# Moving modulation splits, half a query rotation and a recurrence product from VectorE to ScalarE and GpSimd

## The chip, the cores and the metric

The kernel runs on 1 core of one Trainium2 chip. The metric is the device time of the whole program in microseconds (us), the median of three runs. Engines are named as the profile names them: PE (TensorE), PEld (its weight loads), DVE (VectorE), ACT (ScalarE), POOL (GpSimd), SP (SyncE, which issues all DMAs here).

## The reference

Two layers of a hybrid backbone over 256 context tokens and 1024 latent tokens. Cut to what the change touches:

```python
mod = SiLU(cond) @ w_ada + b_ada            # 1024 x 6144 weights, six parts per layer
h   = x * (1 + scale1) + shift1
z   = h @ w_in                              # "in-projection": q, k, v, xr, gr, zm
q   = _rmsnorm(q, q_g); k = _rmsnorm(k, k_g)
# rotary, latent tokens only
o = jnp.stack([x1 * cos - x2 * sin, x1 * sin + x2 * cos], -1)
# RG-LRU, forward and backward, 256 channels
log_a = -RG_C * softplus(-lam) * r          # r, i: sigmoids of two small matmuls of x
a = jnp.exp(log_a)
u = jnp.sqrt(-jnp.expm1(2.0 * log_a)) * i * x
h_t = a_t * h_(t-1) + u_t                   # associative scan
```

After the in-projection come block attention, the out-projection and a feed-forward stage; none of them is edited.

## The kernel before

All matmuls are done in three passes: each fp32 operand is split into a rounded part (`hi`) and the rest (`lo = x - hi`), and PE multiplies hi*hi, hi*lo and lo*hi (`mm3`, L173 to L175). `split` (L165 to L169) does it: a cast on ACT (L165) or DVE (L167), then a subtraction on POOL or DVE (L169).

The in-projection of a layer (`in_proj`) runs groups of columns in turn: xr and gr (the recurrence's input and gate), u and v of the gated MLP, k and v, then q. Three things run beside it as generators that the main line ticks forward:

- **The modulation stream, layer 0 only** (`ada_pe`): parts 2, 3 and 4 of `mod`, 48 slabs `araw` of 128x512 (two 128x256 weight pieces). Each slab is loaded by an SP DMA (L305), split into `ahi` and `alo`, and multiplied on PE (L173 to L175, L318, L319) by a four-column stationary operand. `araw` has two buffers, `ahi` and `alo` three each. The list `ASE` names the engines of the casts and subtractions of even and odd slabs. A new slab's DMA can be issued when the subtraction of the slab two before it has read its buffer.
- **The recurrence** (`lru`, `lru_unit`): per layer, two channel halves with a forward and a backward direction each, and one unit for the context tokens. After the sigmoids `R` and `G` (ACT, L849) come `G*x` on POOL (L855), tanh, exp, square on ACT, `T` on DVE (L866), the root on ACT (L870), `G = G*T` (L873), the scan on DVE (L877), the sum of both directions on POOL (L911) and the output product on DVE (L942). The convolution of the next channel half (L885, L889, tile `xc`, then its split `xh` and `xl`) stands between them on DVE.
- **q and k norms** (`qk_norm`): squares on ACT, a sum and an inverse root on DVE, then `qn` (L1070, from PSUM), the sine products `sq` (L1075, one per block `j` of a pair), the cosine product in place (L1079) and the sum (L1080). q has `nh` = 8 heads (a pair is 128x1024), k has 2. q runs over four latent pairs and one context pair per layer; `q_transpose` (L1137, L1142) follows.

A tile framework reorders the instructions by its own model of durations when the program is built: within an engine they then run in that fixed order. A wait at the head of an engine's queue holds everything behind it.

Of the kernel before, what the change touches and what calls it, by code (L numbers as in the profile page):

```python
# [12 lines left out]
ALU = mybir.AluOpType  # L13
# [44 lines left out]
QCH = ('q',)  # L58
KB = 2
ALAG = 2  # L60
ASE = (('dve', 'dve'), ('act', 'dve'))
XT = 5
CONVR = 0.6
CXP = (16, 17, 18, 19)
# [15 lines left out]
class Kern:  # L80
# [343 lines left out]
    def ada_pe(self, l, parts):  # L424
# [9 lines left out]
        for i in range(len(seq) + ALAG):  # L434
            if i + 1 < len(seq):
                raws.append(load(*seq[i + 1]))
            if i < len(seq):
                raw = raws.pop(0)
                sp.append([self.xs([P, 2, 256], F32R, s=s, bufs=ALAG + 1) for s in ("ahi", "alo")])
                self.split(*sp[-1], raw, *ASE[i % len(ASE)])  # L440
                del raw
# [391 lines left out]
    def lru_unit(self, l, dirs, xc, xh, xl, bd):  # L833

        nc = self.nc
        pf = self.pfm[l]
        bdh, bdl = bd
        RG = []
        for qs in dirs:
            RG.append((self.lx(s="R"), self.lx(s="G")))  # L840
            for gate, dst, bc in ((0, RG[-1][0], C_BA), (1, RG[-1][1], C_BX)):
                for q, cols, _, xs in qs:
                    j = (q * 2 + gate) % bdh.shape[1]
                    n = cols.stop - cols.start
                    for c0 in range(0, n, 512):
                        w = min(512, n - c0)
                        b = self.ps(tag="lg", bufs=2)
                        self.mm3(b[:, :w], bdh[:, j, :], bdl[:, j, :], xh[:, xs][:, c0:c0 + w], xl[:, xs][:, c0:c0 + w], True, True)
                        nc.scalar.activation(dst[:, cols][:, c0:c0 + w], b[:, :w], AF.Sigmoid, bias=pf[:, bc + q:bc + q + 1])  # L849
                        yield 0.6  # L850
        T = []
        for (R, G), qs in zip(RG, dirs):
            T.append(self.lx(s="T"))
            for q, cols, _, xs in qs:
                nc.gpsimd.tensor_tensor(G[:, cols], G[:, cols], xc[:, xs], ALU.mult)  # L855
                nc.scalar.activation(T[-1][:, cols], R[:, cols], AF.Tanh, scale=self.c8[l][:, 1, q:q + 1])
            yield 1.1
        for (R, G), qs in zip(RG, dirs):
            for q, cols, _, xs in qs:
                nc.scalar.activation(R[:, cols], R[:, cols], AF.Exp, scale=self.c8[l][:, 0, q:q + 1])  # L860
            yield 1.1

        for (R, G), t in zip(RG, T):
            sq = self.lx(s="sq")
            nc.scalar.activation(sq, R, AF.Square)
            nc.vector.scalar_tensor_tensor(t, sq, 1.0, t, ALU.add, ALU.mult)  # L866
            del sq
            yield 1.2
        for t in T:
            nc.scalar.activation(t, t, AF.Sqrt)  # L870
            yield 1.0
        for (R, G), t, qs in zip(RG, T, dirs):
            nc.vector.tensor_tensor(G, G, t, ALU.mult)  # L873
            yield 1.1
            for q, cols, init, xs in qs:
                v = [x[:, cols] if q % 2 == 0 else x[:, cols][:, ::-1] for x in (t, R, G)]
                nc.vector.tensor_tensor_scan(v[0], v[1], v[2], init, ALU.mult, ALU.add)  # L877
                yield (cols.stop - cols.start) / 900 + 0.1
        return T
# [173 lines left out]
    def qk_norm(self, bs, nh, gi, rope, t, scale, qn, sq):  # L1053


        nc = self.nc
        tabs, gg = rope
        n = nh * 64
        at = [slice(j * 2 // len(bs), (j + 1) * 2 // len(bs)) for j in range(len(bs))]
        for b, j in zip(bs, at):  # L1060
            nc.scalar.activation(sq[:, j, :], b, AF.Square)
        ss = self.sm([P, 2 * nh], s=f"ss{nh}", bufs=2)
        nc.vector.tensor_reduce(ss, sq.rearrange("p b (h d) -> p (b h) d", d=64), AX.X, ALU.add)

        nc.vector.tensor_scalar(ss, ss, RSC / (64 * scale * scale), RSC * EPS / (scale * scale), ALU.mult, ALU.add)
        r = self.rsqrt(ss, 2 * nh)
        q4 = qn.rearrange("p b (h d) -> p b h d", d=64)
        r4 = r.rearrange("p (b h) -> p b h", h=nh).unsqueeze(3).to_broadcast([P, 2, nh, 64])
        for b, j in zip(bs, at):
            nc.vector.tensor_tensor(q4[:, j], b.rearrange("p b (h d) -> p b h d", d=64), r4[:, j], ALU.mult)  # L1070
        if t >= 2:
            tb = slice((t - 2) * 64, t * 64)
            for j in range(2):
                sn = tabs[gi][:, 1, (t - 2 + j) * 64:(t - 1 + j) * 64].rearrange("p (i two) -> p i two", two=2)
                (nc.vector if j or nh == 2 else nc.gpsimd).tensor_tensor(sq[:, j, :].rearrange("p (h i two) -> p h i two", i=32, two=2),  # L1075
                                        qn[:, j, :].rearrange("p (h i two) -> p h i two", i=32, two=2)[:, :, :, ::-1],
                                        sn.unsqueeze(1).to_broadcast([P, nh, 32, 2]), ALU.mult)
            cs = tabs[gi][:, 0, tb].rearrange("p (b d) -> p b d", d=64).unsqueeze(2).to_broadcast([P, 2, nh, 64])
            nc.vector.tensor_tensor(q4, q4, cs, ALU.mult)  # L1079
            nc.vector.tensor_tensor(qn, qn, sq, ALU.add)  # L1080
        else:
            q3 = qn.rearrange("p b (h d) -> p (b h) d", d=64)
            nc.gpsimd.tensor_tensor(q3, q3, gg[:, gi, :].unsqueeze(1).to_broadcast([P, 2 * nh, 64]), ALU.mult)
        return qn
# [920 lines left out]
```

## Time and profile before

| | |
|---|---|
| median of 3 runs | 3202.53 us (3202.23 to 3202.85) |
| profiled execution | 3198.35 us, its span 3196.6 us |
| PE busy | 2978.1 us, 93% of the span |
| DVE busy | 2297.3 us, 72% |
| POOL busy | 1519.8 us, 48% |
| ACT busy | 1457.5 us, 46% |
| granted TensorE clock, mean | 0.974 |

The in-projections take the stretches from 64 to about 360 us (layer 0; the modulation stream runs from 64 to 220) and from about 1680 to 1905 us (layer 1). Busy shares are averages: what an engine's relief is worth is read from the stage in which it happens, from what PE waits for there. An instruction's duration in the trace includes time in which it had started and could not go on.

### The profile page before, as it was taken

Reading aid. Unit: us, or ns where it says so; the run is one execution under the profiler, and the core shown is the slowest. Engines: PE = TensorE matmul, PEld = TensorE weight load, DVE = VectorE, ACT = ScalarE, POOL = GpSimd, SP = SyncE. Lnnn points to the kernel's source line nnn. Section 1 sums busy time; section 2 is a strip of 40 time slices with the busy share of each in tenths; the row PEclk is TensorE's granted clock in tenths of the full one; section 3 lists DMA queues with packets and bytes.
Section 4 is the critical chain, followed back from the end, with each engine's and each line's share of the span. In section 5 each row is a group of like instructions: output and inputs, shape, how many; then the busy total and the mean of one; then the engine's idle time right before and its main releaser. Section 6 shows DMA issues by size and latency. Waiting matters only on the chain. (4 is left out here: it accounts for less than half of the span.)

```text
span 3196.6 us, 42662 instructions
## 1 busy us (share of the span) xinstructions
PE 2978.1 (93%) x15816; PEld 2487.5 (78%) x15816; DVE 2297.3 (72%) x4582; ACT 1457.5 (46%) x2236; POOL 1519.8 (48%) x850
## 2 busy tenths in 40 slices
PE   7888999999999999999899889999889999999993
PEld 5677789788888888788677868997668888888872
DVE  8879999766676634968664989986755452586859
ACT  5544578744333234332076438883344444433201
POOL 3322244503323227756733214358666666785675
PEclk9999999999999999999999999999989999999996
DMA  7331000235665645442321100004234553544231
GB/s 227 116 94 51 15 1 8 73 108 178 226 235 208 228 160 174 143 132 89 117 106 40 53 25 1 1 24 142 99 111 170 174 182 137 182 155 132 96 119 66
DMA packets 163392, 367.44 MB, mean 115 GB/s; under 512 B 20792, under 2 KB 58440, under 8 KB 163184
## 3 DMA queue, kind: packets, MB, share of 16 engines
q1 hardware_dynamic: 163184, 364.72, 33.5%
q8 instruction: 124, 2.03, 0.3%
q14 instruction: 84, 0.69, 0.1%
HBM read 261.84 MB, written 102.83 MB: 114 GB/s over the span
## 5 line engine op out<-in xcount | busy, mean ns | idle before, releaser
L169 POOL TENSOR_TENSOR wlo<-stg,whi 128x1024 fp32r<-128x1024 f32 (+2 forms) x116 | 240.3, 2084 | 420.8 <-ACT whi L165 381.8
L173 PE MATMUL ps<-hh,whi 128*128 128x512 f32 (+1 forms) x1040 | 376.2, 362 | 5.3 <-ACT htmp L567 4.5
L174 PE MATMUL ps<-hl,whi 128*128 128x512 f32 (+1 forms) x1040 | 374.2, 360 | 4.2 <-POOL hl L387 2.2
L175 PE MATMUL ps<-hh,wlo 128*128 128x512 f32 (+1 forms) x1040 | 373.4, 359 | 0.0
L175 PE MATMUL ps<-wh,ml 128*128 128x512 f32 x840 | 334.6, 398 | 0.0
L173 PE MATMUL ps<-wh,mh 128*128 128x512 f32 x840 | 330.3, 393 | 0.9 <-DVE accy L1749 0.9
L174 PE MATMUL ps<-wl,mh 128*128 128x512 f32 x840 | 330.8, 394 | 0.0
L169 POOL TENSOR_TENSOR pt<-ptf,pt 128x512 fp32r<-128x512 f32 x128 | 166.8, 1304 | 241.9 <-DVE pt L167 224.3
L169 DVE TENSOR_TENSOR ml<-mf,mh 128x1280 fp32r<-128x1280 f32 x84 | 178.2, 2121 | 121.9 <-ACT mh L165 99.2
L1176 DVE TENSOR_SCALAR_CACHE_REDUCE S<-sc 128x512 f32<-128x512 f32 (+1 forms) x416 | 224.8, 582 | 13.5 <-PE pT L1187 11.2
L165 ACT CAST mh<-mf 128x1280 fp32r<-128x1280 f32 x84 | 106.4, 1267 | 278.9 <-PE ps L174 234.7
L174 PEld LDWEIGHTS ps<-hl,whi 128*128 128x128 f32 x1040 | 196.8, 189 | 38.3 <-POOL hl L387 3.9
L173 PEld LDWEIGHTS ps<-hh,whi 128*128 128x128 f32 x1040 | 196.3, 189 | 38.3 <-ACT htmp L567 5.0
L169 POOL TENSOR_TENSOR wl<-wraw,wh 128x1024 fp32r<-128x1024 f32 x60 | 169.8, 2839 | 117.8 <-ACT wh L165 117.7
L175 PEld LDWEIGHTS ps<-hh,wlo 128*128 128x128 f32 x1040 | 197.5, 190 | 32.5
L1179 ACT ACTIVATE S<-S,anm 128x1280 f32<-128x1280 f32 (+1 forms) x160 | 191.2, 1196 | 38.2 <-DVE anm L1178 35.9
L1187 PE MATMUL pT<-ident,S 128*128 128x128 f32 x1344 | 202.2, 274 | 2.0 <-DVE pt L1196 1.4
L1212 PE MATMUL o<-pt,vt 128*128 128x256 f32 x1024 | 192.5, 303 | 9.8 <-POOL pt L169 7.9
L174 PE MATMUL ps<-slo,w1s 128*128 128x512 f32 x448 | 179.6, 401 | 13.8 <-DVE slo L169 13.7
L174 PEld LDWEIGHTS ps<-wl,mh 128*128 128x128 f32 x840 | 157.7, 188 | 40.3
L173 PEld LDWEIGHTS ps<-wh,mh 128*128 128x128 f32 x840 | 157.7, 188 | 39.4 <-DVE accy L1749 2.2
L175 PEld LDWEIGHTS ps<-wh,ml 128*128 128x128 f32 x840 | 157.7, 188 | 37.0
(393 smaller groups left out, 8471.7 us busy)
## 6 DMA issues: line engine op xcount, KB each, us to landing
mf<-mc SPq DMA_DIRECT2D x84, 640.0 KB
mc<-s SPq DMA_DIRECT2D x48, 640.0 KB
aslab<-in_w_ada SPq DMA_DIRECT2D x56, 512.0 KB
stg<-in_w_ff SPq DMA_DIRECT2D x48, 512.0 KB
wraw<-in_w_ff SPq DMA_DIRECT2D x48, 512.0 KB
mc<-f SPq DMA_DIRECT2D x72, 320.0 KB
w1r<-in_w_ff SPq DMA_DIRECT2D x32, 512.0 KB
stg<-in_w_in SPq DMA_DIRECT2D x28, 512.0 KB
```

Of the source, the lines that this page charges most:

```text
L165: nc.scalar.copy(hi, src)
L169: e.tensor_tensor(lo, src, hi.bitcast(F32), ALU.subtract)
L173: mm(out, lh, rh, start=start, stop=False)
L174: mm(out, lh, rl, start=False, stop=False)
L175: mm(out, ll, rh, start=False, stop=stop)
L1176: nc.vector.tensor_scalar(S[:, c0:c0 + n], b[:, :n], 1.0, -3.0e38, ALU.mult, ALU.max, accum_out=u["m"][:, hh, i:i + 1])
L1179: nc.scalar.activation(S[:, :c0], S[:, :c0], AF.Exp, bias=u["nm"][:, hh:hh + 1], accum_out=u["d"]["den"][:, ci % 2, hh:hh + 1])
L1187: nc.tensor.transpose(b[:, c, hh, :], u["S"][hh][:, (2 * j + c) * P:(2 * j + c + 1) * P], self.ident)
L1212: nc.tensor.matmul(o, v, pt[:, hl, c, :], start=j == 0 and c == 0 and hl == 0, stop=j == last and c == 1 and hl == 1)
```

## The change

Three edits. The modulation splits: even slabs are cast on ACT and subtracted on POOL (before: both on DVE); odd slabs stay as they were, cast on ACT and subtracted on DVE. The recurrence's product `G*T` goes from DVE to POOL in both layers. In the q rotation, the sine product of a pair's second block goes to POOL, where the first block's already was, and the sum is halved: the first block on POOL, the second on DVE. k is as before.

```diff
-ASE = (('dve', 'dve'), ('act', 'dve'))
+ASE = (('act', 'pool'), ('act', 'dve'))
...
         for (R, G), t, qs in zip(RG, T, dirs):
-            nc.vector.tensor_tensor(G, G, t, ALU.mult)
+            nc.gpsimd.tensor_tensor(G, G, t, ALU.mult)
...
-                (nc.vector if j or nh == 2 else nc.gpsimd).tensor_tensor(sq[:, j, :].rearrange("p (h i two) -> p h i two", i=32, two=2),
+                (nc.vector if nh == 2 else nc.gpsimd).tensor_tensor(sq[:, j, :].rearrange("p (h i two) -> p h i two", i=32, two=2),
...
-            nc.vector.tensor_tensor(qn, qn, sq, ALU.add)
+            if nh == 2:
+                nc.vector.tensor_tensor(qn, qn, sq, ALU.add)
+            else:
+                for e, j in ((nc.gpsimd, 0), (nc.vector, 1)):
+                    e.tensor_tensor(qn[:, j, :], qn[:, j, :], sq[:, j, :], ALU.add)
```

Since the framework orders the instructions anew, more moves than the diff names. Lines from L1083 on have numbers higher by 4 in the changed kernel.

POOL, layer 0, in the middle of the modulation stream (`wlo`: low part of in-projection weights; `xl`: low part of the convolution's result). Before:

```order
L169 TENSOR_TENSOR xl_885<-xc_799,xh_884 128x1024
L855 TENSOR_TENSOR G_898<-G_898,xc_799 128x1024
L169 TENSOR_TENSOR wlo_1266<-stg_784,whi_1265 128x1024
L855 TENSOR_TENSOR G_977<-G_977,xc_799 128x1024
L169 TENSOR_TENSOR wlo_1492<-stg_997,whi_1491 128x1024
L911 TENSOR_TENSOR T_1092<-T_1092,T_1122 128x1024
```

In the changed kernel, the same stretch from the second `G*x` on:

```order
L855 TENSOR_TENSOR G_977<-G_977,xc_799 128x1024
L169 TENSOR_TENSOR alo_1107<-araw_1083,ahi_1106 128x512
L169 TENSOR_TENSOR alo_1148<-araw_1125,ahi_1147 128x512
L169 TENSOR_TENSOR alo_1192<-araw_1165,ahi_1191 128x512
L873 TENSOR_TENSOR G_898<-G_898,T_1092 128x1024
L169 TENSOR_TENSOR alo_1230<-araw_1207,ahi_1229 128x512
L873 TENSOR_TENSOR G_977<-G_977,T_1122 128x1024
L911 TENSOR_TENSOR T_1092<-T_1092,T_1122 128x1024
L169 TENSOR_TENSOR alo_1278<-araw_1245,ahi_1277 128x512
L169 TENSOR_TENSOR wlo_1492<-stg_997,whi_1491 128x1024
```

The subtractions of the even slabs now stand between the recurrence's instructions; `alo_1278` stands behind L911, which needs the results of both scans on DVE.

DVE, layer 1, the first channel half's scans beside the convolution of the second half (`gr`, `cx`, `ug`: gate and MLP evacuations from PSUM banks `ps`). Before:

```order
L873 TENSOR_TENSOR G_15556<-G_15556,T_15649 128x1024
L205 SCALAR_TENSOR_TENSOR gr_15506<-gr_15506,ps_15699 128x512
L877 SCALAR_TENSOR_TENSOR T_15649<-R_15555,pfm_90,G_15556 128x1024
L873 TENSOR_TENSOR G_15593<-G_15593,T_15669 128x1024
L889 SCALAR_TENSOR_TENSOR xc_15814<-xr_15283,pfm_90,xc_15814 128x1023
L207 SCALAR_TENSOR_TENSOR gr_15506<-gr_15506,ps_15699 128x512
L205 SCALAR_TENSOR_TENSOR cx_15284<-cx_15284,ps_15739 128x256
L877 SCALAR_TENSOR_TENSOR T_15669<-R_15592,pfm_90,G_15593 128x1024
L207 SCALAR_TENSOR_TENSOR cx_15284<-cx_15284,ps_15739 128x256
L205 SCALAR_TENSOR_TENSOR ug_15770<-ug_15770,ps_15773 128x512
L889 SCALAR_TENSOR_TENSOR xc_15814<-xr_15283,pfm_90,xc_15814 128x1022
L942 SCALAR_TENSOR_TENSOR T_15649<-T_15649,gr_15505 128x1024
```

In the changed kernel:

```order
L877 SCALAR_TENSOR_TENSOR T_15653<-R_15559,pfm_90,G_15560 128x1024
L205 SCALAR_TENSOR_TENSOR gr_15510<-gr_15510,ps_15703 128x512
L877 SCALAR_TENSOR_TENSOR T_15673<-R_15596,pfm_90,G_15597 128x1024
L889 SCALAR_TENSOR_TENSOR xc_15818<-xr_15287,pfm_90,xc_15818 128x1023
L942 SCALAR_TENSOR_TENSOR T_15653<-T_15653,gr_15509 128x1024
L207 SCALAR_TENSOR_TENSOR gr_15510<-gr_15510,ps_15703 128x512
L205 SCALAR_TENSOR_TENSOR cx_15288<-cx_15288,ps_15743 128x256
L889 SCALAR_TENSOR_TENSOR xc_15818<-xr_15287,pfm_90,xc_15818 128x1022
```

Both products are gone, the second scan stands earlier, and L942, which needs POOL's L911, moved from behind the convolution's last step to two evacuations and that step's front.

DVE, layer 0, the last latent q pair. Before:

```order
L1070 TENSOR_TENSOR qn_3415<-ps_3380,rsy_566_3422 128x512
L1075 TENSOR_TENSOR sq_564_3416<-qn_3415,rtab_469_2643 128x512
L1142 TENSOR_TENSOR qT_3466<-qps_3467,qT_3466 64x4x128
L1079 TENSOR_TENSOR qn_3415<-qn_3415,rtab_469_2643 128x1024
L1142 TENSOR_TENSOR qT_3466<-qps_3467,qT_3466 64x4x128
L1080 TENSOR_TENSOR qn_3415<-qn_3415,sq_564_3416 128x1024
```

In the changed kernel:

```order
L1070 TENSOR_TENSOR qn_3418<-ps_3383,rsy_566_3425 128x512
L1146 TENSOR_TENSOR qT_3470<-qps_3471,qT_3470 64x4x128
L1079 TENSOR_TENSOR qn_3418<-qn_3418,rtab_469_2643 128x1024
L1146 TENSOR_TENSOR qT_3470<-qps_3471,qT_3470 64x4x128
L1084 TENSOR_TENSOR qn_3418<-qn_3418,sq_564_3419 128x512
```

The sine product left DVE, the cosine product now waits for two sine products of POOL, and the sum on DVE is half as wide.

## Rows read from the trace of the kernel before

**Rows 1.** Busy time by stage: window, length, busy (instructions), PE clock, DMA share, GB/s.

```profile
64.00:220.00 156.00, 131.82 (x778) 100.34 (x776) 122.86 (x167) 79.20 (x112) 47.29 (x21) 0.97 0.38 118
1760.00:1850.00 90.00, 75.22 (x531) 70.11 (x530) 85.51 (x271) 37.85 (x72) 23.44 (x18) 0.92 0.17 53
```

**Rows 2.** PE's waits, 64 to 220 us: total us, times, longest.

```profile
PE ada L318 <- DVE ahi L167: 8.8, 6, 2.6
PE ada L319 <- DVE alo L169: 3.0, 4, 1.3
PE adaf L326 <- DVE arow L461: 3.0, 3, 1.4
...
PE ada L174 <- DVE alo L169: 1.5, 2, 1.1
```

**Rows 3.** Slabs `araw`: instructions, duration min/median/max in ns, first and last start.

```profile
L305 SPq DMA_DIRECT2D araw<-in_w_ada x48: 367/368/546, 64.4 to 210.2; - x48
L169 DVE TENSOR_TENSOR alo<-araw,ahi x48: 654/691/2895, 74.4 to 217.4; 128x512 fp32r<-128x512 f32 x48
L167 DVE CAST ahi<-araw x24: 389/427/2640, 72.9 to 212.5; 128x512 fp32r<-128x512 f32 x24
L165 ACT CAST ahi<-araw x24: 600/618/623, 73.8 to 214.7; 128x512 fp32r<-128x512 f32 x24
```

**Rows 4.** SP's queue, 157 to 163 us: start, duration, issue (two slabs apart).

```profile
158.14 0.37 SPq L305 DMA_DIRECT2D araw<-in_w_ada  x1
...
162.13 0.37 SPq L305 DMA_DIRECT2D araw<-in_w_ada  x1
```

**Rows 5.** Groups by form, 64 to 220 us: busy us, mean ns, idle before and releasers.

```profile
L169 DVE TENSOR_TENSOR alo<-araw,ahi 128x512 fp32r<-128x512 f32 x48 | 44.1, 925 | 12.3 <-ACT ahi L165 11.9
...
L167 DVE CAST ahi<-araw 128x512 fp32r<-128x512 f32 x24 | 19.3, 802 | 11.3 <-DMA araw<-in_w_ada 9.7 <-PE ada L175 1.2
...
L855 POOL TENSOR_TENSOR G<-G,xc 128x1024 f32<-128x1024 f32 x4 | 9.8, 2440 | 34.5 <-ACT G L849 34.5
...
L873 DVE TENSOR_TENSOR G<-G,T 128x1024 f32<-128x1024 f32 x4 | 4.8, 1208 | 0.0
```

**Rows 6.** Timeline at 1794 us: start, duration, engine, instruction, idle before and releaser.

```profile
1794.45 2.35 POOL L169 TENSOR_TENSOR wlo<-stg,whi 128x1024 fp32r<-128x1024 f32 x1 [4.80 <-ACT whi L165]
1794.52 2.29 DVE L198 SCALAR_TENSOR_TENSOR rsy<-rst,rsy 128x2 f32<-128x2 f32 x1
```

**Rows 7.** Timeline, layer 1, first channel half's scans, 1710.5 to 1726 us.

```profile
1710.85 2.41 POOL L169 TENSOR_TENSOR wlo<-stg,whi 128x1024 fp32r<-128x1024 f32 x1 [5.02 <-ACT whi L165]
...
1711.20 4.20 DVE L877 TENSOR_TENSOR_SCAN T<-R,pfm,G 128x1024 f32<-128x1024 f32 x1
...
1718.57 2.34 DVE L877 TENSOR_TENSOR_SCAN T<-R,pfm,G 128x1024 f32<-128x1024 f32 x1
...
1721.05 2.38 POOL L911 TENSOR_TENSOR T<-T,T 128x1024 f32<-128x1024 f32 x1 [7.79 <-DVE T L877]
...
1721.74 2.78 DVE L889 SCALAR_TENSOR_TENSOR xc<-xr,pfm,xc 128x1022 f32<-128x1022 f32 x1
...
1724.44 1.21 DVE L942 SCALAR_TENSOR_TENSOR T<-T,gr 128x1024 f32<-128x1024 f32 x1
...
1725.64 0.51 PE L173 MATMUL ps<-xh,bdh 128*128 128x512 f32 x1 [2.90 <-ACT xh L165]
```

**Rows 8.** Timeline of the last latent q pair, layer 0, 349 to 356 us.

```profile
349.90 1.28 POOL L1075 TENSOR_TENSOR sq<-qn,rtab 128x512 f32<-128x512 f32 x1 [11.41 <-DVE qn L1070]
...
350.38 1.34 DVE L1075 TENSOR_TENSOR sq<-qn,rtab 128x512 f32<-128x512 f32 x1
...
352.48 1.23 DVE L1079 TENSOR_TENSOR qn<-qn,rtab 128x1024 f32<-128x1024 f32 x1
...
354.46 1.23 DVE L1080 TENSOR_TENSOR qn<-qn,sq 128x1024 f32<-128x1024 f32 x1
...
355.83 0.41 PE L1137 MATMUL qps<-ident,qn 128*128 128x128 f32 x2 [0.41 <-DVE qn L1080]
```

## The prediction

> **What bounds the kernel now.** I read the table of engines first: PE is busy 93% of the span, DVE 72%, so every microsecond gained or lost must come out of the 7% in which PE idles. Then the busy time by stage, since the edits act in two stretches only. In the modulation stretch (64 to 220 us) PE works 131.82 of 156 us and DVE 122.86, POOL only 47.29 [rows 1]: PE idles 24 us there, and DVE has 33 us left. In the middle of layer 1's in-projection (1760 to 1850) DVE works 85.51 of 90 us while PE has 75.22 [rows 1]: DVE is the fuller engine there. Third, PE's waits: in the modulation stretch 8.8 + 3.0 + 3.0 + 1.5 = 16.3 us end with a cast, a subtraction or the row sums of DVE [rows 2]. That is all that the first edit can win there through DVE. The stream itself also has to be looked at as a loop: 48 loads start between 64.4 and 210.2 us, 47 steps of 3.10 us, so one buffer turns over in 6.2 us [rows 3]. Where nothing disturbs it, a turn takes 162.13 - 158.14 = 3.99 us [rows 4]. So the buffers aren't the pace at present; casts and subtractions that come late are.
>
> Last, how DVE and POOL stand to each other, for two edits of three move work from the one to the other. At 1794.45 POOL starts a subtraction of 2.35 us, and at 1794.52 DVE starts an operation on 2 columns that takes 2.29 us [rows 6]: it ends when POOL's does. The scan at 1711.20 takes 4.20 us beside POOL's 2.41, and 2.34 later without [rows 7]. Such DVE operations wait out the POOL operation. The same shows in bulk: the 48 `alo` have a median of 0.69 us [rows 3] and a mean of 0.925 [rows 5], the 24 `ahi` 0.43 and 0.80. The excess is 44.1 - 48 x 0.69 = 11.0 and 19.3 - 24 x 0.43 = 9.0, together 20.0 us for 47.29 us of POOL work: DVE loses at least 0.42 us per us of POOL on these two groups alone.
>
> **The change part by part.** All terms are against the profiled execution's own 3198.35 us, 0.13% below the median of 3202.53; I add the 4.2 us at the end.
>
> *1. Modulation stretch.* Taken off DVE: 24 casts x 0.43 + 24 subtractions x 0.69 + 4 products x 1.21 = 10.3 + 16.6 + 4.8 = 31.7 us, at undisturbed durations [rows 3, 5]. Put on POOL: a subtraction of 128x512 isn't there on POOL before; by half of the 128x1024 rows (2.41 and 2.44, [rows 5, 7]) 1.2, and by the same width in the q rotation 1.28 [rows 8]; I take 1.28. So 24 x 1.28 + 4 x 2.44 = 40.5 us, and POOL goes from 47 to 88 of 156 us. What this takes back from DVE: at 0.42 per us 17 us, at one for one 40.5. I take 25, nearer the lower end because DVE isn't always there to be blocked, so DVE's net relief is about 7 us instead of 31.7. ACT gets 24 casts x 0.62 = 15 us more on 79 of 156; it has room.
>
> The even slabs pay for it: a cast of 0.62 for 0.43 and a subtraction of 1.28 for 0.69 make their way 0.8 us longer, 24 x 0.8 = 19 us if this length were the pace. It mostly isn't: 3.99 + 0.8 is still under 6.2. But POOL runs its list in order: in the new order four subtractions stand among the G products, and `alo_1278` stands behind the sum of directions, which waits for both scans; before, POOL idled 34.5 us ahead of its G products, waiting for sigmoids [rows 5], and nothing that PE needed soon stood behind them. Now slabs do. A late slab holds its `araw` buffer, the next load sits at the head of SP's queue, and weight loads sit behind it. Bounds: -16.3 (every wait of PE on DVE goes, nothing new) to +19 (the longer turn is the pace). Between them: the relief net of blocking is 7 of 31.7, so I credit 16.3 x 7/31.7 = -3.6; for new waits behind POOL's list I charge five late slabs at 1.28, +6.4, a choice. I take **+2**.
>
> *2. Layer 1's recurrence.* G*T takes 2.44 on POOL instead of 1.21 on DVE [rows 5]. The chain of a channel half is root, two products, two scans, sum, output product; the products now run one after the other on POOL, 4.88 for 2.42, and each also blocks the convolution steps or the first scan on DVE meanwhile: +2.4 on the chain. In the first half it then matters what stands ahead of what. Before, the last convolution step ran 1721.74 to 1724.52, stretched to 2.78 by the sum on POOL (2.38), and L942 came after it; the cast follows and PE waits 2.90 us for `xh` at 1725.64 [rows 7]. In the new order L942 stands ahead of that step: 1.21 us, and with it its wait for the sum on POOL, which the step before only overlapped. Together +2.4 + 1.2, with the step no longer stretched (1.28 instead of 2.78, -1.5 at most) but pushed behind the sum (up to 2.38): 0 to +6, I take +4. The second half falls in the stretch where DVE is 95% busy; there DVE gets 2.4 us back and the chain gets 2.4 longer: 0 to +3.5, and below zero if DVE's fill is what counts (-2.4); I take +2. The context unit, 128x256 columns, a quarter of it: +0.5. Sum **+6.5** (-3 to +10).
>
> *3. Layer 0's recurrence* lies within term 1; its context unit +0.5 (-1.2 to +1.2).
>
> *4. q rotation, eight latent pairs.* Before, DVE: sine product 1.34 (stretched, for POOL's 1.28 runs beside it), cosine 1.23, sum 1.23 [rows 8]. Now POOL has two sines, 2.56, from 349.90 to 352.5. The cosine, in place on the whole pair, must wait for both: it ran at 352.48 anyway, behind two other DVE steps [rows 8]. So nothing is lost there. The POOL half of the sum takes about 1.28 for DVE's half of about 0.65 (half of 1.23), and blocks it if it starts first: the pair ends 354.46 + 1.28 + (0 to 0.65), 355.7 to 356.4 against 355.69. Three pairs of four in a layer don't stand with PE behind them; the last does, PE waits 0.41 there already [rows 8]. DVE gains 1.34 + 0.6 a pair, which the next evacuations may use, and the first pair of a layer has no DVE steps to cover the second sine (+1.3). Per layer +1, both **+2** (-2 to +5).
>
> Sum: 2 + 6.5 + 0.5 + 2 = +11, so 3209.4 on the profiled execution's footing and **3213** on the median's.
>
> A rule of the Trainium skill ("SBUF — State Buffer", Who interferes with whom) speaks against this change: a DVE operation with two SBUF inputs and a GpSimd operation that reads SBUF exclude each other, and the second one blocks until the first has finished. The rows on the scan and on the 2-column operation agree. By it in its hardest form (every POOL microsecond taken from DVE) term 1's relief would be 31.7 - 40.5 = -9 us, a loss.
>
> **The rivals.** (a) *Faster.* The waits of PE on DVE in the modulation stretch are the only ones to go, and POOL's subtractions hide in its idle time. For it: PE's three longest groups of waits there all name DVE, and POOL's idle time is 109 us. Against: the 0.42 per us. Price: 0.7 x 16.3 = -11.4, and half of the rest (9/2 = +4.5): -7, 3196 on the median's footing. (b) *No change.* Relief and blocking cancel, and layer 1's longer chain falls into gaps in which DVE idles: within 6 us of 3202.5. For it: all terms are a few us and of both signs. (c) *Slower by much more.* The even slabs' longer way becomes the pace, since each late slab delays SP's whole queue: +19 + 9 = +28, 3230. It decides from the point at which an even slab's turn, 4.8 us undisturbed, comes to more than 6.2 us through POOL's list, so from 1.4 us of mean wait on POOL. (d) *Full blocking.* If each added POOL us costs DVE a us, DVE has 122.86 + 9 = 132 of 156 us to do, as full as PE; PE's waits on DVE grow from 16.3 by about those 9, and the sum becomes +9 + 9 = +18, 3220. The rule of the Trainium skill told above comes to this.
>
> **How the numbers follow.** Two runs of this kernel differ by less than 0.2% (6.4 us), about what a measurement can tell from no change. Chances: the forecast of 3213 with its neighbourhood, 0.31; (d) 0.10; (c) 0.06; (b) 0.28; (a) 0.25. Slower is the sum of the first three, 0.47; same 0.28; faster 0.25. The range must reach into (a) and most of (c): leaving out the part of (a) below 3190 (some 0.1) and the part of (c) beyond 3230 (some 0.05), it is 3190 to 3230. The forecast's own range is 3205 to 3221.
>
> **What the changed profile would show.** Term 1: `alo` on DVE keeps a mean well over 0.69, at 0.9 or more, though half of them are gone; PE's waits for `ada` name POOL's `alo` or ACT's `ahi` where they named DVE's; the 48 loads take about as long from first to last as before (145.8 us). Loads done by 200 us would mean (a); by 225 (c). Term 2: the wait of PE for `xh` in layer 1, 2.90 before, rises to 5 to 7, and L942 stands ahead of the last convolution step. Term 4: the last pair's first transpose waits 0.4 to 1.2 us for the sum. It would be wrong if the two stretches changed little and another stage moved, or if DVE's idle time grew without PE's waits falling.

## The result, and the profile after

The changed kernel takes 3221.84 us in the median of four runs (3220.93 to 3224.45). The medians of four runs each lie 3221.84 - 3202.38 = 19.5 us apart. The ratio to the kernel before, over runs on the same chip, is 1.0071 with a 95% interval of 1.0059 to 1.0084: slower by 0.6 to 0.7%, some 20 us. The forecast was 3213, slower, with a range of 3190 to 3230. The direction was right, the size was about half of what was measured, and most of the half that was missing stands in layer 0, as PE time for the same matmuls.

| | before | after |
|---|---|---|
| span of the profiled execution | 3196.6 us | 3219.2 us |
| PE busy | 2978.1 | 2990.5 |
| DVE busy | 2297.3 | 2266.6 |
| ACT busy | 1457.5 | 1471.1 |
| POOL busy | 1519.8 | 1608.5 |
| granted TensorE clock, mean | 0.974 | 0.968 |

DVE was indeed relieved, and POOL took the work. Where the time went is found by asking when the same matmuls run in both traces. The first score matmul of layer 0 starts at 356.2 us before and at 372.3 after: +16.1 us in layer 0's in-projection. From the 8200th matmul, near the end of layer 0, to the first score matmul of layer 1 it is 275.9 us before and 282.6 after: +6.7. The rest is +4.0 between the two stretches and -3.4 from the second to the last matmul. These two also differ by +2 to +5 and by -0.2 to -4.4 in most runs below, whatever their edit, so they belong for the most part to the single execution that was profiled before, not to the change.

Layer 0's stretch in three pieces, first of the kernel before, then of the changed one (window, length, busy time of PE, PEld, DVE, ACT and POOL, granted clock, DMA share, GB/s):

```profile
64.00:160.00 96.00, 81.46 (x447) 59.82 (x446) 80.92 (x97) 50.72 (x73) 34.78 (x16) 0.98 0.38 120
160.00:260.00 100.00, 86.34 (x605) 75.26 (x604) 78.00 (x208) 42.83 (x62) 19.45 (x11) 0.95 0.30 90
260.00:356.20 96.20, 81.56 (x424) 67.31 (x423) 87.92 (x244) 37.08 (x76) 19.87 (x17) 0.96 0.12 38
sum 292.20, PE 249.37 PEld 202.38 DVE 246.83 ACT 130.63 POOL 74.10; mean PE 83.12 PEld 67.46 DVE 82.28 ACT 43.54 POOL 24.70
```

```profile
64.00:160.00 96.00, 78.04 (x401) 56.51 (x399) 59.80 (x59) 53.39 (x80) 56.83 (x29) 0.93 0.36 112
160.00:260.00 100.00, 82.19 (x544) 69.04 (x542) 67.69 (x151) 49.36 (x73) 40.03 (x24) 0.91 0.28 83
260.00:372.30 112.30, 100.24 (x526) 83.98 (x527) 95.51 (x280) 41.44 (x84) 33.24 (x27) 0.92 0.15 45
sum 308.30, PE 260.48 PEld 209.53 DVE 222.99 ACT 144.19 POOL 130.10; mean PE 86.83 PEld 69.84 DVE 74.33 ACT 48.06 POOL 43.37
```

PE's idle time grew from 292.20 - 249.37 = 42.8 us to 308.30 - 260.48 = 47.8: **+5.0**. PE's busy time for the same matmuls grew from 249.37 to 260.48: **+11.1**, and the mean granted clock beside it, between 0.95 and 0.98 in the three pieces before, lies between 0.91 and 0.93. So two thirds of the loss in layer 0 aren't waits. They are matmuls at the lower of the clock's two levels, 1.2 instead of 2.4 GHz, after waits. An estimate from these rows: a piece of mean clock 0.93 spends 14% of its time at the lower level, which makes some 49 us of the stretch, for some 22 before; half of the 27 us more is 14 us, and PE wasn't busy in all of them.

One such place, 130 to 150 us, where the clock was 1.00 in both windows before:

```profile
130.00:140.00 10.00, 6.53 (x36) 5.29 (x37) 10.00 (x5) 4.00 (x7) 5.43 (x3) 0.83 0.17 52
140.00:150.00 10.00, 6.19 (x22) 4.02 (x21) 8.69 (x11) 2.80 (x6) 8.30 (x4) 0.66 0.38 105
```

The timeline of that place in the changed kernel (start, duration, engine, instruction, idle before and its releaser):

```profile
128.10 2.36 POOL L873 TENSOR_TENSOR G<-G,T 128x1024 f32<-128x1024 f32 x1 [2.05 <-ACT T L870]
128.22 3.33 DVE L889 SCALAR_TENSOR_TENSOR xc<-xr,pfm,xc 128x1023 f32<-128x1023 f32 x1
130.42 2.24 POOL L169 TENSOR_TENSOR alo<-araw,ahi 128x512 fp32r<-128x512 f32 x1
131.47 1.74 DVE L169 TENSOR_TENSOR alo<-araw,ahi 128x512 fp32r<-128x512 f32 x1
132.62 2.81 POOL L873 TENSOR_TENSOR G<-G,T 128x1024 f32<-128x1024 f32 x1
133.13 4.45 DVE L877 TENSOR_TENSOR_SCAN T<-R,pfm,G 128x1024 f32<-128x1024 f32 x1
133.26 0.38 PE L319 MATMUL ada<-alo,s 128*4 128x256 f32 x1 [3.82 <-DVE alo L169]
...
142.12 2.23 DVE L169 TENSOR_TENSOR alo<-araw,ahi 128x512 fp32r<-128x512 f32 x1
...
144.40 0.38 PE L319 MATMUL ada<-alo,s 128*4 128x256 f32 x1 [3.81 <-DVE alo L169]
```

The convolution step takes 3.33 us where it takes 1.27 undisturbed, because POOL's G*T started 0.12 us before it. POOL's slab then takes 2.24 instead of 1.29, DVE's slab 1.74 instead of 0.69, the scan 4.45 instead of 2.34. Each engine waits out the other, and the slab that PE needs stands at the end of the row. PE waits 3.82 us, and again 3.81; the clock of the two windows is 0.83 and 0.66.

PE's waits in the stretch, against [rows 2]; they are read to 240 us, since the stream now runs to 235:

```profile
PE ada L319 <- DVE alo L169: 13.5, 5, 4.5
PE ada L319 <- POOL alo L169: 5.9, 7, 1.9
PE ada L174 <- POOL alo L169: 4.9, 2, 4.3
PE adaf L326 <- DVE arow L461: 3.4, 2, 2.6
```

Before, the longest of them was 2.6 us; now five waits on DVE's `alo` come to 13.5, and the waits on a DVE cast are gone. All of PE's waits on DVE in these rows come to 16.9 us, against the 16.3 of before, and 10.8 on POOL are new. The slabs, against [rows 3], and the subtractions by form, against [rows 5]:

```profile
L305 SPq DMA_DIRECT2D araw<-in_w_ada x48: 367/368/629, 64.3 to 223.5; - x48
```

```profile
L169 POOL TENSOR_TENSOR alo<-araw,ahi 128x512 fp32r<-128x512 f32 x24 | 34.7, 1446 | 49.5 <-ACT ahi L165 44.2 <-PE ps L174 4.1 <-PE ada L319 1.2
L169 DVE TENSOR_TENSOR alo<-araw,ahi 128x512 fp32r<-128x512 f32 x24 | 26.7, 1113 | 27.8 <-ACT ahi L165 27.7
```

The last load starts 13 us later than before. The subtractions of the odd slabs, which stayed on DVE, take 1.11 us on the mean; the same ones took 0.99 before (0.925 is the mean of odd and even).

In layer 1 the dearest place is the second channel half:

```profile
1781.25 2.60 POOL L873 TENSOR_TENSOR G<-G,T 128x1024 f32<-128x1024 f32 x1 [1.71 <-ACT T L870]
1781.52 4.48 DVE L877 TENSOR_TENSOR_SCAN T<-R,pfm,G 128x1024 f32<-128x1024 f32 x1
1787.13 0.62 ACT L165 CAST xcs<-xcc 128x512 fp32r<-128x512 f32 x1 [5.54 <-DVE xcc L889]
1787.62 2.34 DVE L877 TENSOR_TENSOR_SCAN T<-R,pfm,G 128x1024 f32<-128x1024 f32 x1
1787.83 3.20 POOL L169 TENSOR_TENSOR xcs<-xcc,xcs 128x512 fp32r<-128x512 f32 x1 [3.98 <-ACT xcs L165]
...
1790.99 2.38 POOL L911 TENSOR_TENSOR T<-T,T 128x1024 f32<-128x1024 f32 x1
...
1793.40 1.22 DVE L942 SCALAR_TENSOR_TENSOR T<-T,gr 128x1024 f32<-128x1024 f32 x1 [2.86 <-POOL T L911]
...
1801.04 0.58 PE L173 MATMUL mixps<-ws,vh 128*128 128x256 f32 x1 [7.93 <-ACT vh L165]
```

The scan waits out G*T (4.48), the next scan holds POOL's `xcs` (3.20 for some 1.27), the sum L911 stands behind that, and DVE idles 2.86 us at L942. Behind L942 stand all the small steps that normalise `v`, and PE waits 7.93 us for `vh`, where before no wait for it was longer than 1.9:

```profile
PE mixps L173 <- ACT vh L165: 3.3, 2, 1.9
```

Part of this is the new order: before, two evacuations of `v` and the first of its statistics ran ahead of L942 (1769.15 to 1771.82), in the changed kernel the statistics run behind it.

### The profile page after: what moved, and what is told of

Same layout as the page of the kernel before. It is cut to its first block, busy times and chain, and to the rows that moved or that the text cites. A ratio compares the mean times of both kernels' runs of the same rounds, so it can differ in the third digit from the quotient of the medians.

```text
span 3219.2 us, 42708 instructions
## 1 busy us (share of the span) xinstructions
PE 2990.5 (93%) x15816; PEld 2498.0 (78%) x15816; DVE 2266.6 (70%) x4516; ACT 1471.1 (46%) x2260; POOL 1608.5 (50%) x900
## 5 line engine op out<-in xcount | busy, mean ns | idle before, releaser
L173 PE MATMUL ps<-hh,whi 128*128 128x512 f32 (+1 forms) x1040 | 377.8, 364 | 11.2 <-DVE gr L207 5.2
```

Source lines behind the costliest of these rows:

```text
L173: mm(out, lh, rh, start=start, stop=False)
```

## The experiments

Each was timed in five runs or more against the kernel before on the same chip. The table splits each profiled execution as above: layer 0 up to the first score matmul, and layer 1 from the 8200th matmul to its first score matmul, both as differences from the kernel before, with PE's idle part of layer 0 (from 64 us) beside it. The remainder of layer 0 is PE's busy time for the same matmuls.

| run | ratio (95%) | layer 0, us | of it idle | layer 1, us |
|---|---|---|---|---|
| the change (four runs) | 1.0071 (1.0059 to 1.0084) | +16.1 | +5.0 | +6.7 |
| e1_split | 1.0043 (1.0030 to 1.0055) | +11.2 | +4.8 | +0.5 |
| e2_gt | 1.0043 (1.0030 to 1.0055) | +2.8 | -0.9 | +7.1 |
| e3_q | 0.9999 (0.9989 to 1.0009) | -0.6 | +0.8 | +0.4 |
| e5_act_only | 0.9993 (0.9984 to 1.0002) | -5.6 | -5.0 | -2.2 |
| d1_gdummy | 1.0061 (1.0048 to 1.0074) | +12.2 | +8.8 | +8.2 |
| d4_sdummy | 1.0000 (0.9991 to 1.0008) | +0.1 | -1.9 | +0.5 |
| d5_split_3buf | 0.9996 (0.9987 to 1.0005) | -1.9 | -3.1 | -1.1 |
| d6_act_q | 0.9984 (0.9975 to 0.9993) | -3.2 | -4.3 | -1.5 |
| g1_3buf | 0.9964 (0.9952 to 0.9977) | -11.7 | -7.1 | -1.9 |
| g2_all_3buf | 1.0036 (1.0023 to 1.0048) | +6.7 | +4.1 | +6.6 |
| g3_act_q_3buf | 0.9967 (0.9954 to 0.9979) | -10.9 | -9.8 | -1.4 |
| g4_gmemset | 1.0019 (1.0010 to 1.0028) | +3.6 | +2.9 | -0.2 |

Execution to execution a stage moves by a few us (the stretch between the two, which no edit touches, by up to 5); a single entry of the stages is no better than that, and the ratios decide. The tile framework orders every version anew, so each run has its edit and a new order in it, and no run separates the two.

**Which of the three edits.** First edit alone, second alone, third alone:

```diff
-ASE = (('dve', 'dve'), ('act', 'dve'))
+ASE = (('act', 'pool'), ('act', 'dve'))
```

> Only the first edit: even modulation slabs cast on ACT and subtracted on POOL; G*T and the q rotation as before. Theory A (the products G*T on POOL are what blocks DVE in the recurrence, and the late slabs stand behind those blocked steps): without G*T on POOL the modulation stretch loses little, +3 us of the whole (0 to +6), and layer 1 is as before. Theory B (the slabs' subtractions in POOL's fixed order are late by themselves): nearly all of layer 0's loss, +16 us at the start of block attention, is there, total +14 to +17.

```diff
-            nc.vector.tensor_tensor(G, G, t, ALU.mult)
+            nc.gpsimd.tensor_tensor(G, G, t, ALU.mult)
```

> Only the second edit: G*T on POOL in both layers; splits and q rotation as before. Theory A: the scans and convolution steps of DVE wait out the 2.4 us products, about +6 us in layer 0 and +8 in layer 1, total +14. Theory B: layer 0 unchanged within 2 us, layer 1 +8, total +8.

```diff
-                (nc.vector if j or nh == 2 else nc.gpsimd).tensor_tensor(sq[:, j, :].rearrange("p (h i two) -> p h i two", i=32, two=2),
+                (nc.vector if nh == 2 else nc.gpsimd).tensor_tensor(sq[:, j, :].rearrange("p (h i two) -> p h i two", i=32, two=2),
...
+                for e, j in ((nc.gpsimd, 0), (nc.vector, 1)):
+                    e.tensor_tensor(qn[:, j, :], qn[:, j, :], sq[:, j, :], ALU.add)
```

> Only the third edit: both sine products of a q pair on POOL, the sum halved between POOL and DVE. Both theories: within 3 us of before, since PE waits for q at the first and last pairs only (0.9 and 1.1 us in the changed kernel, 1.0 and 0.8 before). A third theory C (the q edit reorders DVE and POOL so that the k norms and value evacuations ahead of q come late, as the waits at 296.8, 303.6 and 312.3 in the changed kernel may say): +4 to +8.

The first costs 0.43%, nearly all in layer 0. The second costs 0.43%, most of it in layer 1. The third costs nothing: theory C falls. The two add up to 0.86%; within their intervals that is the whole change's 0.71%. Theory A had +3 us for the first edit and theory B no loss of layer 0 to the second; B comes near for the first edit and A for the second, and each falls for the other, so the two edits were taken further apart.

**The first edit.** One half of it: casts on ACT, subtractions left on DVE.

```diff
-ASE = (('dve', 'dve'), ('act', 'dve'))
+ASE = (('act', 'dve'), ('act', 'dve'))
```

> Half of the first edit: even slabs cast on ACT as in the change, but subtracted on DVE as before, so POOL gets nothing. If POOL is the cause (theories A and B), DVE is 10 us freer at no price and the time falls by 0 to 5 us. If ACT's queue is the cause (its list in order, a cast 0.2 us longer), the slabs come late here too: +3 to +8.

The interval includes no change, and the profile has layer 0 5.6 us shorter. ACT's queue isn't the cause, then; the subtraction on POOL is (1.0043 against 0.9993). It could cost by blocking DVE or by being waited for. So this version was given POOL operations that nobody waits for:

```diff
+                if i % 2 == 0:
+                    z = self.xs([P, 2, 256], s="zs", bufs=1)
+                    lo = sp[-1][1].bitcast(F32)
+                    nc.gpsimd.tensor_tensor(z, lo, lo, ALU.mult)
```

> Even slabs cast on ACT and subtracted on DVE, as in the run before that gave no difference; in addition POOL squares each even slab's finished low part into a scratch tile that nobody reads: 24 operations of 128x512 that block without being waited for. If the first edit costs through blocking, +5 to +12 us. If it costs because PE waits for a subtraction that stands in POOL's list and takes 1.3 us there, -3 to +3 us.

1.0000 against 0.9993: blocking, as far as these 24 operations stand for it, costs some 2 us, of a first edit of 13.8. The two intervals overlap, so the 2 us can't be told from none, and the single profiles, 5.7 us apart in layer 0, leave room for more. The operations read one tile, and take 1.04 us instead of 1.29, so they block somewhat less. What remains, 1.0043 against 1.0000, comes with the subtraction being on POOL and waited for there. The trace agrees: over the 24 even slabs, from the end of the cast to the end of the subtraction it is 1.31 us on the mean before, 2.08 with the first edit alone and 2.11 in the whole change. With the first edit alone the operation itself makes 0.58 of these 0.77 us (1.44 for 0.86 on the mean, 1.29 for 0.69 in the median), and 0.20 is a later start. A few slabs bear much of that, through their position in POOL's list, as the first slab that PE waits for, in the changed kernel:

```profile
81.45 3.38 POOL L169 TENSOR_TENSOR bdl<-bd,bdh 128x1024 fp32r<-128x1024 f32 x1
84.80 2.83 POOL L169 TENSOR_TENSOR xl<-xc,xh 128x1024 fp32r<-128x1024 f32 x1
87.59 1.26 POOL L169 TENSOR_TENSOR alo<-araw,ahi 128x512 fp32r<-128x512 f32 x1
...
88.90 0.38 PE L174 MATMUL ada<-alo,s 128*2 128x256 f32 x1 [4.27 <-POOL alo L169]
```

That PE's new waits come from these 0.8 us is read from the names of the waits; how much of the 13.8 us each part makes, no run shows.

Then the buffers, which the prediction's rival (c) spoke of. In the first edit, the whole change, and the kernel before as the control:

```diff
-        load = lambda part, blk, k: self.ada_load(l, part, blk * 256, k, lambda s: self.xs([P, 2, 256], s=s, bufs=2), "araw")
+        load = lambda part, blk, k: self.ada_load(l, part, blk * 256, k, lambda s: self.xs([P, 2, 256], s=s, bufs=3), "araw")
```

> The first edit alone with three araw buffers for two. If the longer turn of an even slab's buffer paces the stream (rival c of the prediction), the +12 us of the first edit fall to +4 or less. If late subtractions are the cause, which a buffer more doesn't make earlier, +9 to +13.

> The kernel before with three araw buffers for two and nothing else: the control for the run of the first edit with three buffers (0.9996). If the buffers bind only where a slab's turn is longer (the first edit), 0 to -3 us here. If they bind before already, -8 to -13 us, and the first edit would then still cost its 12 us against a kernel with equal buffers.

> The whole change with three araw buffers. If the first edit costs through the buffers alone and the second through blocking and POOL's list around the scans, the 22 us of the whole fall to what the second costs by itself: +9 to +14. If G*T on POOL also cost through late slabs, whose buffers it holds, less: +5 to +8 (layer 1's +7 alone).

By the run of the first edit alone rival (c) seemed proven: the loss was gone (0.9996). The control says otherwise. Three buffers make the kernel before 0.36% faster as well, so against a kernel with equal buffers the first edit still costs 0.32% of its 0.43%: the buffers account for about a quarter of it at most, and the difference of 0.11% is less than the intervals can tell from nothing. The whole change falls from +0.71% to +0.36%, and against the control it still loses 0.72%. What the control shows is that two buffers held back the kernel before too:

```profile
L305 SPq DMA_DIRECT2D araw<-in_w_ada x48: 367/368/462, 64.1 to 183.7; - x48
```

The 48 loads run in 119.6 us instead of 145.8.

**The second edit.** It could cost by a longer chain (the product takes 2.4 us instead of 1.2) or by blocking. The product was put back on DVE and POOL given one of the same size that nobody reads:

```diff
             nc.vector.tensor_tensor(G, G, t, ALU.mult)
+            z = self.XL.tile([P, D], F32, tag="zz", name=self.nm("zz"), bufs=1)
+            nc.gpsimd.tensor_tensor(z, G, R, ALU.mult)
```

> The product G*T stays on DVE as before; behind it POOL multiplies the finished G by R into a scratch tile that nobody reads, so POOL gets ten operations of the size of the moved ones, and no chain grows longer by them. If the second edit costs through blocking (DVE steps that wait out POOL's products), most of its +13.8 us comes back, +7 to +14, and the scan's mean stays above 3 us. If it costs because the product stands on the chain root - product - scan at 2.4 instead of 1.2 us, -1 to +4 us.

It costs more than the edit itself, 0.61%. In layer 1 it costs about the same (+8.2 against +7.1), in layer 0 far more (+12.2 against +2.8); there it stands for more than the edit. In layer 1 the second channel half shows it cleanest, since DVE has the same order there as before. Before:

```profile
1758.88 2.35 DVE L877 TENSOR_TENSOR_SCAN T<-R,pfm,G 128x1024 f32<-128x1024 f32 x1
1763.97 2.35 DVE L877 TENSOR_TENSOR_SCAN T<-R,pfm,G 128x1024 f32<-128x1024 f32 x1
1769.94 0.38 PE L173 MATMUL ps<-xcs,bdh 128*128 128x256 f32 x1 [0.79 <-ACT xcs L165]
```

With the added product:

```profile
1774.92 2.58 POOL L875 TENSOR_TENSOR zz<-G,R 128x1024 f32<-128x1024 f32 x1 [3.79 <-DVE G L873]
1775.15 4.50 DVE L879 TENSOR_TENSOR_SCAN T<-R,pfm,G 128x1024 f32<-128x1024 f32 x1
1782.03 2.40 POOL L875 TENSOR_TENSOR zz<-G,R 128x1024 f32<-128x1024 f32 x1 [4.53 <-DVE G L873]
1782.40 4.17 DVE L879 TENSOR_TENSOR_SCAN T<-R,pfm,G 128x1024 f32<-128x1024 f32 x1
1790.19 0.58 PE L173 MATMUL ps<-xcs,bdh 128*128 128x256 f32 x1 [4.71 <-ACT xcs L165]
```

Each scan starts 0.2 to 0.4 us behind POOL's product and ends about when the product and its own 2.35 us have passed one after the other. The two scans take 4.0 us longer, and PE, which waits for `xcs` behind them, waits 3.9 us longer. (The first scan of the first half proves nothing here: it took 4.20 us before as well, beside `wlo` [rows 7].) But POOL's list is longer too, so the same was run with an operation that waits for the same G, keeps POOL busy about as long, and reads only one column:

```diff
-            nc.gpsimd.tensor_tensor(z, G, R, ALU.mult)
+            nc.gpsimd.tensor_copy(z[:, 0:1], G[:, 0:1])
+            nc.gpsimd.memset(z, 0.0)
+            nc.gpsimd.memset(z, 1.0)
```

> Like the run with POOL's product of G and R behind G*T on DVE (1.0061), but POOL fills the scratch tile twice with a constant instead, behind a copy of one column of G, so that its list waits for the same and is busy about as long, without reading rows that DVE's two-input operations contend for. If that run cost through DVE and POOL excluding each other, 0 to +5 us here and scans of 2.3 us. If it cost through POOL's list (what stands behind the waiting operation), +12 to +19 again.

0.19%, some 6 us, just above the 0 to +5 expected of blocking and far from +12 to +19; in layer 1 it is nothing (-0.2). In its trace the first of these scans takes its 2.35 us beside two fills, and PE waits 0.7 us for `xcs`:

```profile
1767.16 2.35 DVE L881 TENSOR_TENSOR_SCAN T<-R,pfm,G 128x1024 f32<-128x1024 f32 x1
1767.34 0.95 POOL L876 MEMSET zz<- 128x1024 f32 x1
1768.35 0.96 POOL L877 MEMSET zz<- 128x1024 f32 x1
```

So some two thirds of the added product's cost (0.42 of 0.61%) come from its reading SBUF beside a DVE operation with two inputs there, and the rest (0.19%; in layer 1 nothing) from POOL's list and the new order. The fills and the copy keep POOL busy somewhat shorter, 2.1 us for 2.4, so the split is rough. The Trainium skill ("SBUF — State Buffer", Who interferes with whom) has this: a DVE operation with two SBUF inputs contends with a GpSimd operation that reads SBUF, not with one that only writes it. Both halves agree with these rows.

**A faster version.** The relief of DVE without new POOL operations beside slabs and scans, with two and with three buffers; the diffs are those of e5_act_only and e3_q, and the second has the buffers' too:

> Every slab cast on ACT and subtracted on DVE, with the third edit (q rotation), and G*T on DVE: what relieves DVE without new operations of POOL next to the scans and slabs. If the two edits that cost are both costs of POOL beside DVE, this is the best version: -2 to -7 us. If it is within 2 us of before, DVE's relief is worth nothing here.

> Casts of all slabs on ACT, subtractions on DVE, the third edit, and three araw buffers: what was at 0.9984 with two buffers. If the stream still waits for buffers there (DMA named ahead of 22 us of ACT's idle time), -3 to -6 us more; if not, within 2 us of the run with two.

With two buffers it is 0.16% (5 us) faster than before, as expected where POOL beside DVE is what costs. With three, 0.9967 is no better than three buffers alone (0.9964). The fastest version measured is the kernel before with a third `araw` buffer: -11 us.

## Why the prediction was right or wrong

**What bounds the kernel.** "So the buffers aren't the pace at present" was wrong. The step that failed compared a turn of 6.2 us with an undisturbed one of 3.99 [rows 4], as if disturbed turns were no part of the pace. In [rows 5] stood the hint: the DVE casts idled 9.7 us for `araw` loads. A third buffer gives 11 us (g1_3buf).

**Term 1** (+2 predicted; +11.2 in layer 0 with the edit alone). Mis-sized was the whole. Its currency was PE's waits, and of these 4.8 us came with the edit alone. The five late slabs charged at 6.4 us were too few: PE's waits for POOL's subtractions come to 10.8 us in the changed kernel, in nine waits. The credit of 3.6 us for waits on DVE wasn't there either (16.9 us after, 16.3 before). The 0.8 us by which an even slab's way was to grow is there (1.31 to 2.08 us). What the sum had no term for is the clock: the new waits of some 4 us are followed by matmuls at the lower level, and PE's time for the same matmuls grows by 6.4 us with the edit alone and by 11.1 in the whole change. "DVE's net relief" as a lever failed too: a version that takes the casts off DVE (e5_act_only) at no price on POOL gains at most 0.16%. What PE waits for is single late slabs, not DVE's load. That the term had the right sign is in part luck: it was a choice between -16.3 and +19.

**Term 2** (+6.5 predicted). Right in sum: +7.1 in layer 1 with the edit alone (e2_gt), +6.7 in the whole. Its parts fell elsewhere. In the first half "+2.4 on the chain" isn't there: from the end of the root to the end of the second scan it is 12.75 us (1726.63 to 1739.38), before 12.77 (1708.14 to 1720.91). What is there is L942 ahead of the last convolution step, with its wait for POOL's sum, as foreseen: the cast of `xh` starts 19.5 us behind the root instead of 16.4. But PE no longer waits for `xh`; it waits ahead of it for a PSUM bank that DVE's `gr` evacuation, behind L942, holds:

```profile
1742.78 1.23 DVE L942 SCALAR_TENSOR_TENSOR T<-T,gr 128x1024 f32<-128x1024 f32 x1 [2.23 <-POOL T L911]
```

```profile
PE ps L173 <- DVE gr L207: 5.2, 1, 5.2
```

With the wait behind it that is 5.22 + 1.12 against 2.90 + 1.94 before, +1.5 where +4 was expected. The larger part is the 7.93 at `vh`, in the second half, where +2 was: there the chain is longer, by 2.6 us from the first root to the end of the second scan, and the scan stretched by POOL's product (4.48 for 2.35) is most of that. So the right sum is in part luck. d1_gdummy shows that blocking alone, with the product at 1.2 us on DVE, can cost as much; how much of the change's own 7 us is blocking, the longer product or the new order isn't shown. In layer 0 the edit alone gave +2.8, where term 3 had +0.5.

**Term 4** (+2 predicted): 0 (e3_q). That nothing is lost at the cosine held: in the last pair of layer 0 it idles 1.40 us for POOL's second sine, but starts 3.41 us behind the evacuation, before 3.42. The sum was to end later; on two engines it is ready earlier, since POOL's half runs while DVE still evacuates `qT`:

```profile
366.71 2.54 POOL L1075 TENSOR_TENSOR sq<-qn,rtab 128x512 f32<-128x512 f32 x2 [7.35 <-DVE qn L1070]
369.28 1.22 DVE L1079 TENSOR_TENSOR qn<-qn,rtab 128x1024 f32<-128x1024 f32 x1 [1.40 <-POOL sq L1075]
370.58 1.30 POOL L1084 TENSOR_TENSOR qn<-qn,sq 128x512 f32<-128x512 f32 x1 [1.34 <-DVE qn L1079]
371.26 1.17 DVE L1084 TENSOR_TENSOR qn<-qn,sq 128x512 f32<-128x512 f32 x1
```

From the evacuation to the first transpose it is 365.87 to 371.94, 6.07 us; before, 349.06 to 355.83, 6.77.

**The rivals.** (b) and (a) fell with the sign; in (a), PE's waits on DVE falling away, those on DVE casts went, and 13.5 us on DVE's subtractions came, where 3.0 + 1.5 had been. (d), full blocking, with a chance of 0.10, gave 3220 and came nearest to the time, 3221.84, which lies just above the forecast's own range of 3205 to 3221; its mechanism is what the added product shows, but for the first edit blocking was worth some 2 us only. (c) had the right object, late slabs that hold buffers and SP's queue, and gave 3230. Its sign, loads done by 225 us, came (the last starts at 223.5), but its condition didn't: it needed 1.4 us of mean wait on POOL, and the even slabs start there 0.66 us behind their cast. Its buffers account for a quarter of the first edit at most. The prediction's 0.2% between two runs was too narrow as well: on one chip the kernel before ran from 3191.95 to 3205.64 us.

## What to carry to other kernels

Where POOL and DVE both read two operands from SBUF, work that moves from the one to the other need not come off DVE's path: it can come back as a wait at the next such operation, as beside G*T here. A result that an engine waits for also comes later from the slower POOL, as the slabs did. Each of these two cost 0.43%; in the q rotation, where PE hardly waits for the result, the same kind of move cost nothing (0.9999). A wait that a change adds on PE may bring a lower clock behind it. In layer 0 here that cost twice the wait itself (+11.1 us beside +5.0); in layer 1, where PE idles 7.8 us more, its time for the same matmuls even fell by 1.1, so it isn't a fixed price. And a buffer that seems wide enough by its undisturbed turn can still be the limit: an experiment that adds one needs the same buffer in the kernel before, or it proves too much.

## What the runs showed of the hardware

POOL's fills of 128x1024 took 0.95 to 1.11 us (g4_gmemset), and no 128x1024 scan beside one was stretched (2.34 to 2.35 us). POOL itself waits when DVE is first: the added product took 2.35 us at best and up to 6.50 (d1_gdummy). An operation that waits so shows it in its own duration, as the 3.33 us of the convolution step that takes 1.27. What the clock cost is in PE's time for the same matmuls: 11.1 of the +16.1 us in layer 0.
